# Two stacked transformer blocks on one core: 1/rms of the queries and of the compressed vectors applied behind the products

## Chip, cores and metric

The kernel runs on one core of one Trainium2 chip. The metric is device time in microseconds (us) of one execution. Engines are named as in the profile: PE is TensorE's matrix products, PEld its weight loads, DVE is VectorE, ACT is ScalarE, POOL is GpSimd, SP issues the loads of weights.

## The reference, cut to what matters

Two blocks of two layers each are computed in fp32. The first block has two streams of 256 tokens (context and latent). The change lies in its mixer:

```python
u = h @ w_in
u_q, u_k, u_v, u_cq, u_ckv, u_kr, pool_in = jnp.split(u, offs, axis=-1)
qg = rms_norm(u_q.reshape(b, l, GQA_HEADS, HEAD_DIM), g_q_gqa)          # 6 heads of 64
kg = rms_norm(u_k.reshape(b, l, GQA_KV_HEADS, HEAD_DIM), g_k_gqa)       # 2 heads of 64
qm = (rms_norm(u_cq, g_cq) @ w_uq).reshape(b, l, MLA_HEADS, MLA_QK)     # 256 -> 6 x 96
kv = (rms_norm(u_ckv, g_ckv) @ w_ukv).reshape(b, l, MLA_HEADS, MLA_NOPE + MLA_V)
km = jnp.concatenate([kv[..., :MLA_NOPE], k_rope], axis=-1)
qm, km = rms_norm(qm, g_q_mla), rms_norm(km, g_k_mla)
...            # rotation of latent queries and keys, then
p = softmax(q k^T * scale); o = p v        # GQA heads and MLA heads
```

`rms_norm(x, g)` is x times 1/sqrt(mean(x^2) + eps) times g, per token and head. In layer 0 both streams have queries, in layer 1 only the latent one; keys and values always come from both.

## The kernel before

Activations lie with tokens on the 128 partitions (four tiles: two of context, two latent) and are transposed on TensorE for the next product. Every fp32 weight is loaded by SP into one of five `raw` buffers, split by ScalarE (`wh`, L345) and VectorE (`wl`, L346) into a high and a low part in a ring of four, and each product is three matmuls (`mm3`, L428 to L430) on such parts. Sums go to two PSUM buffers of two banks each (`acc`), transposes and small products to two single banks (`wk`) and one pair (`pr`).

Side work runs as Python generators (`spawn`, `tick`, `drain`): the main line of products calls `tick` after each weight part, and each tick lets the generators issue their next piece. The order of issue is also the priority by which the framework's planner then orders the instructions of each engine; an instruction is placed when its inputs and buffers are ready in the planner's own model of time.

`first_layer` runs for both layers of the first block. `in_group` computes three column groups of the input projection: keys, values and the compressed vectors `ckv` (416 columns), queries (448), compressed queries `cq` (448). Its inner `ev` copies sums from PSUM with ScalarE (L832, L833) to token tiles `u` (`uin` in the profile). Four generators follow:

- `chain_kv`: square sums of each key head (GpSimd squares, L463, VectorE sums, L464) and of `ckv` (ScalarE, L454), the power -1/2 on GpSimd (L436), the multiply of keys (L760) and of `ckv` (L761) by 1/rms, the rotation, the transposes (L775, L776) and the split of `ckv` (`ckr`).
- `chain_q`: the same for the queries: square sums, 1/rms (24 columns in layer 0, by twelve small VectorE operations L439 to L444; 12 columns in layer 1, by GpSimd), multiply L790, rotation or gain (L794), transposes L799, copy L801.
- `chain_cq`: square sums of the compressed queries (L454), 1/rms (L436), multiply L811, transposes L817, the split into `cqr` (L423, L424).
- `chain_km`: up_kv makes keys and values of the MLA heads from `ckr` (copies L874, L876); the chain takes square sums, one 24-column 1/rms, multiplies by it (L889) and by the gain (L895, L893), and transposes (L902).

`latent_queries` makes the MLA queries from `cqr` in two banks for each tile of tokens; `chain_uq` copies them out (L923), squares them (L463), multiplies by 1/rms (L934) and by the gain (L935), rotates and transposes (L945). `attention` runs 18 pairs of heads in layer 0 (six of them with four softmax pieces, twelve with two) and 12 in layer 1 (two pieces each), three pairs deep: scores (L998), the negative maximum (L1008), exponentials with their sum (L1011), reciprocal and scaling (L1013, L1015), transposes (L1024, copy L1027), the product with the values (L1037), the split of the result (`mix`, L419, L420). The second block's attention already scales its scores in the softmax (L1565, L1569).

## Time and profile before

| what | value |
|---|---|
| median of 3 runs | 1771.93 us (1769.02 to 1772.63) |
| the profiled execution | 1766.66 us |
| its span, first to last instruction | 1764.7 us |
| granted TensorE clock, mean of the span | 0.984 of full speed |
| busy: PE, DVE, ACT, POOL | 1694.5, 1025.4, 855.8, 331.6 us |

The prediction works with durations from the one profiled execution; its own time lies 5.27 us under the median of the three runs. In the profile the mixer of layer 0 lies between about 60 and 215 us, that of layer 1 between about 705 and 830 us.

### The profile page before, as it was taken

The page shows a single profiled execution, that of the slowest core. Times are in us where ns is not written, and L with a number is a line of the kernel's source. Part 1 is how long each engine was busy: PE and PEld are TensorE (multiplying, and loading weights), DVE is VectorE, ACT ScalarE, POOL GpSimd, SP SyncE. Part 2 cuts the span into 40 slices and gives each one's busy share as a digit, 9 for nine tenths or more (in the row PEclk, how much of TensorE's full clock was granted, in tenths as well). Part 3 has the DMA queues.
Part 4 walks back from the last instruction along what each step waited for, and adds up shares of the span by engine and source line. Part 5 has one row for each costly group of instructions (what it writes and reads, how often), then busy time and mean ns, then how long its engine had stood idle before and what let it go on. Part 6 is the DMA issues. An engine that isn't in the chain of part 4 may idle for free.

```text
span 1764.7 us, 26533 instructions
## 1 busy us (share of the span) xinstructions
PE 1694.5 (96%) x10062; PEld 1362.7 (77%) x10062; DVE 1025.4 (58%) x1882; ACT 855.8 (48%) x1658; POOL 331.6 (19%) x414
## 2 busy tenths in 40 slices
PE   6989999999999999889999999999999999999998
PEld 5776578777778888656899978877778788787787
DVE  3476634333333436774566778776575577866755
ACT  4556534413222234564544465665554446655542
POOL 1134110211112121331122224520000034300000
PEclk9999999999999999999999999999999999999999
DMA  7611254555443322602665545444355444343453
GB/s 285 211 61 54 74 190 125 179 163 166 149 151 118 96 78 77 219 30 81 218 189 184 188 146 167 138 132 156 119 170 188 145 155 154 129 160 119 155 183 104
DMA packets 71999, 256.23 MB, mean 145 GB/s; under 512 B 8120, under 2 KB 9272, under 8 KB 71616
## 3 DMA queue, kind: packets, MB, share of 16 engines
q1 hardware_dynamic: 71856, 254.53, 44.2%
q8 instruction: 79, 1.29, 0.3%
q14 instruction: 48, 0.39, 0.1%
q10 hardware_dynamic: 16, 0.02, 0.0%
HBM read 253.47 MB, written 1.05 MB: 144 GB/s over the span
## 4 chain that ended last, share of the span: by engine, by line
PE 86%; DVE 6%; ACT 3%; DMA 2%; POOL 2%; issue 1%; SPq 0%; DVEq 0%; ACTq 0%; POOLq 0%
PE acc L428 24%; PE acc L430 23%; PE acc L429 23%; PE acc L998 2%; DVE wl L346 2%; PE pr L549 2%; PE wk L1037 1%; DMA raw<-in_dram 1%; PE pr L1024 1%; ACT e L1011 1%; PE pr L1703 1%; PE wk L549 1%; ACT wh L345 1%; PE pr L1553 1%; DVE nmx L1008 1%
## 5 line engine op out<-in xcount | busy, mean ns | idle before, releaser
L346 DVE TENSOR_TENSOR wl<-raw,wh 128x1024 fp32r<-128x1024 f32 (+3 forms) x384 | 478.7, 1249 | 415.5 <-ACT wh L345 414.9
L345 ACT CAST wh<-raw 128x1024 fp32r<-128x1024 f32 (+3 forms) x384 | 396.7, 1034 | 505.2 <-PE acc L430 338.6
L428 PE MATMUL acc<-wl,hh 128*128 128x512 f32 x576 | 231.1, 401 | 4.6 <-ACT tga L1683 2.3
L429 PE MATMUL acc<-wh,hh 128*128 128x512 f32 x576 | 230.5, 400 | 0.0
L430 PE MATMUL acc<-wh,hl 128*128 128x512 f32 x576 | 229.6, 399 | 0.0
L428 PE MATMUL acc<-wl,hidh 128*128 128x512 f32 x384 | 152.5, 398 | 0.0
L429 PE MATMUL acc<-wh,hidh 128*128 128x512 f32 x384 | 151.2, 394 | 0.0
L430 PE MATMUL acc<-wh,hidl 128*128 128x512 f32 x384 | 151.0, 395 | 0.0
L1197 POOL TENSOR_TENSOR sqr<-relu 128x512 f32<-128x512 f32 (+1 forms) x64 | 72.6, 1135 | 346.5 <-ACT relu L1195 233.1
L428 PEld LDWEIGHTS acc<-wl,hh 128*128 128x128 f32 x576 | 109.5, 190 | 28.2 <-ACT tga L1683 3.2
L430 PEld LDWEIGHTS acc<-wh,hl 128*128 128x128 f32 x576 | 109.5, 190 | 22.8 <-issue 1.3
L429 PEld LDWEIGHTS acc<-wh,hh 128*128 128x128 f32 x576 | 109.5, 190 | 22.2 <-issue 1.3
L428 PE MATMUL acc<-hl,wh 128*128 128x258 f32 (+1 forms) x384 | 113.1, 295 | 3.5 <-DVE xc L1627 3.5
L429 PE MATMUL acc<-hh,wh 128*128 128x258 f32 (+1 forms) x384 | 111.6, 291 | 0.0
L430 PE MATMUL acc<-hh,wl 128*128 128x258 f32 (+1 forms) x384 | 111.0, 290 | 0.0
L428 PE MATMUL acc<-h2l,wh 128*128 128x512 f32 (+1 forms) x288 | 108.4, 376 | 2.7 <-DVE dx L1128 2.7
L429 PE MATMUL acc<-h2h,wh 128*128 128x512 f32 (+1 forms) x288 | 108.5, 377 | 0.0
L430 PE MATMUL acc<-h2h,wl 128*128 128x512 f32 (+1 forms) x288 | 107.5, 373 | 0.0
L428 PEld LDWEIGHTS acc<-wl,hidh 128*128 128x128 f32 x384 | 72.2, 188 | 17.8 <-issue 1.8
L430 PEld LDWEIGHTS acc<-wh,hidl 128*128 128x128 f32 x384 | 72.1, 188 | 17.1 <-issue 1.0
L429 PEld LDWEIGHTS acc<-wh,hidh 128*128 128x128 f32 x384 | 72.2, 188 | 16.4 <-issue 0.8
L1130 POOL TENSOR_TENSOR x<-x,dx 128x512 f32<-128x512 f32 x30 | 45.8, 1553 | 198.1 <-DVE dx L1128 198.1
(425 smaller groups left out, 3343.1 us busy)
## 6 DMA issues: line engine op xcount, KB each, us to landing
raw<-in_dram SPq DMA_DIRECT2D x448, 512.0 KB, 3.6
raw<-in_dram SPq DMA_DIRECT2D x16, 448.0 KB, 4.2
raw<-in_dram SPq DMA_DIRECT2D x8, 416.0 KB, 6.0
x<-in_dram SPq DMA_DIRECT2D x2, 1024.0 KB
band<-in_dram SPq DMA_DIRECT2D x4, 512.0 KB
raw<-in_dram SPq DMA_DIRECT2D x4, 288.0 KB, 4.2
out_dram<-x SPq DMA_DIRECT2D x4, 256.0 KB, 2.0
rows<-in_dram SPq DMA_DIRECT2D x4, 232.0 KB, 2.5
```

Source lines behind the costliest of these rows:

```text
L345: S.copy(h, src)
L346: V.tensor_tensor(l, src, h.bitcast(F32), ALU.subtract)
L428: T.matmul(ps, a[0], b[1], start=start, stop=False)
L429: T.matmul(ps, a[0], b[0], start=False, stop=False)
L430: T.matmul(ps, a[1], b[0], start=False, stop=stop)
L549: T.matmul(ps[32 * j:32 * j + 32, 0:P], cpad[:, k, :], raw[:, k * P:(k + 1) * P], start=a == 0, stop=a == 1)
L998: T.matmul(ps[:, a, s_ * w:(s_ + 1) * w], pr["q"][a][s_], pr["k"][a], start=True, stop=True)
L1008: V.tensor_reduce(nmx, ps.rearrange("p a (q w) -> p (a q) w", q=nq), AX.X, ALU.max, negate=True)
L1011: S.activation(e[:, c * w:(c + 1) * w], pf[:, c * w:(c + 1) * w], AF.Exp, bias=nmx[:, c:c + 1], accum_out=ssum[:, c:c + 1])
L1024: T.transpose(pt[:, a, (k * nq + s_) * P:(k * nq + s_ + 1) * P], d["e"][:, a * 512 + (s_ * nk + k) * P:a * 512 + (s_ * nk + k + 1) * P], i ...
L1130: (V if o else G).tensor_tensor(xs, xs, d, ALU.add)
L1197: G.tensor_tensor(s, t, t, ALU.mult)
```

## The change

1/rms of the queries (GQA and MLA) is no longer multiplied into them. It is kept in `rq` and `rm` and enters the softmax: the negative maximum is multiplied by it, and the exponential takes it as its scale. 1/rms of the compressed queries cancels in the norm of the MLA queries up to the epsilon; it scales the squares of the query products (`rcq`) and the final `rm`. 1/rms of `ckv` (now the last of the columns 33 to 35 of `krs`) is applied where the keys and values are copied out of PSUM. So the transposes of `cq` and `ckv` need only the copies out of PSUM. The nope part of the MLA key gain moves into the query gain `gqm`. Query products are multiplied by `gqm` straight out of PSUM by VectorE, and squares move from GpSimd to ScalarE; the keys' 1/rms of the MLA heads is taken tile by tile on GpSimd. `rsqrt` and `rsqrt_mean` get an argument for the place of the result, and `head_pairs`, `gqa_pairs` and `mla_pairs` hand each pair its columns of `rq` or `rm` as `pr["r"]`.

```diff
-        krs = const.tile([P, 4, 33], F32, tag="krs", name=nm("krs"))
+        krs = const.tile([P, 4, 36], F32, tag="krs", name=nm("krs"))
+        rqs = smp.tile([P, 52], F32, tag="rq", name=nm("rqs"), bufs=1)
+        rq, rm = (rqs[:, a:a + 24].rearrange("p (t h) -> p t h", t=4) for a in (0, 24))
+        rcq = rqs[:, 48:52]
...
+        V.tensor_tensor(gqm[:, 0:64], gqm[:, 0:64], rw("gkm", 96)[:, 0:64], ALU.mult)
...
         def chain_kv(us, j0=0):
...
-                group_ss(s3[:, j - j0, 0:2], u[:, 0:128], 2, u[:, 128:256])
+                group_ss(s3[:, j - j0, 0:2], u[:, 0:128], 2, u[:, 128:256], act=True)
...
-            r = rsqrt(ms.rearrange("p t c -> p (t c)"), 3 * n).rearrange("p (t c) -> p t c", t=n)
+            for j, u in enumerate(us, j0):
+                pt = wk_ps()
+                T.transpose(pt[:, 0:P], u[:, 256:384], ident)
+                scaled_split(ckh[:, j * P:(j + 1) * P], ckl[:, j * P:(j + 1) * P], pt[:, 0:P], gk)
+            r = krs[:, j0:j0 + n, 33:36]
+            G.tensor_tensor(r, s3, nhalf[:, 0:3 * n].rearrange("p (t c) -> p t c", t=n), ALU.pow)
             yield 1
...
-                V.tensor_scalar(u[:, 256:384], u[:, 256:384], r[:, j - j0, 2:3], None, ALU.mult)
...
-                T.transpose(pt[:, P:2 * P], u[:, 256:384], ident)
                 V.tensor_copy(kT[:, j * P:(j + 1) * P], pt[:, 0:P])
-                scaled_split(ckh[:, j * P:(j + 1) * P], ckl[:, j * P:(j + 1) * P], pt[:, P:2 * P], gk)
                 yield 1
+
+        def ev_q(j, ps, u):
+
+            p3 = ps[:, 0:384].rearrange("p (g d) -> p g d", g=6)
+            if tq[j] >= 2:
+                S.copy(u[:, 0:384], ps[:, 0:384])
+            else:
+                V.tensor_tensor(u[:, 0:384].rearrange("p (g d) -> p g d", g=6), p3, gq8.unsqueeze(1).to_broadcast([P, 6, 64]), ALU.mult)
+            S.activation(Bqf[:, j * 384:(j + 1) * 384], ps[:, 0:384], AF.Square)
 
         def chain_q(us):
...
-                group_ss(ss[:, 6 * j:6 * j + 6], u[:, 0:384], 6, Bqf[:, j * 384:(j + 1) * 384])
+                V.tensor_reduce(ss[:, 6 * j:6 * j + 6], Bqf[:, j * 384:(j + 1) * 384].rearrange("p (g d) -> p g d", g=6), AX.X, ALU.add)
             yield 1
-            r = rsqrt_mean(ss, 6 * n, 64)
             for j, u in enumerate(us):
                 u3 = u[:, 0:384].rearrange("p (g d) -> p g d", g=6)
-                V.tensor_tensor(u3, u3, r[:, 6 * j:6 * j + 6].unsqueeze(2).to_broadcast([P, 6, 64]), ALU.mult)
                 if tq[j] >= 2:
                     rope_tok(u3, u3, 6, 32, pair(qs[:, tq[j] - 2, 0, 0, :]), pair(qs[:, tq[j] - 2, 0, 1, :]))
-                else:
-                    G.tensor_tensor(u3, u3, gq8.unsqueeze(1).to_broadcast([P, 6, 64]), ALU.mult)
-                yield 1
+                    yield 1
...
+            rsqrt_mean(ss, 6 * n, 64, rq[:, tq[0]:tq[0] + n, :].rearrange("p t h -> p (t h)"))
 
         def chain_cq(us):
...
-            for j, u in enumerate(us):
-                sumsq(ss[:, j:j + 1], u[:, 0:256], u[:, 256:512])
-            r = rsqrt_mean(ss, n, 256)
-            for j, u in enumerate(us):
-                V.tensor_scalar(u[:, 0:256], u[:, 0:256], r[:, j:j + 1], None, ALU.mult)
-            yield 1
...
+                sumsq(ss[:, j:j + 1], u[:, 0:256], u[:, 256:512])
                 yield 1
+            rsqrt_mean(ss, n, 256, rcq[:, tq[0]:tq[0] + n])
...
-                S.copy(u, pk[:, 0:384])
+                S.activation(u, pk[:, 0:384], AF.Copy, scale=krs[:, t, 35:36])
                 uks.append(u)
-                S.copy(vm[:, t, :], pv[:, 0:384])
+                S.activation(vm[:, t, :], pv[:, 0:384], AF.Copy, scale=krs[:, t, 35:36])
             W.used()
 
         def chain_km():
-            ss = sm(24, "ssm")
+            rs_ = []
             for j, u in enumerate(uks):
-                group_ss(ss[:, 6 * j:6 * j + 6], u, 6)
-                V.tensor_scalar(ss[:, 6 * j:6 * j + 6], ss[:, 6 * j:6 * j + 6], krs[:, j, 32:33], None, ALU.add)
-                yield 1
-            r = rsqrt_mean(ss, 24, 96)
-            yield 2
+                ss = sm(6, "ssm")
+                group_ss(ss, u, 6, act=True)
+                V.tensor_scalar(ss, ss, krs[:, j, 32:33], 1.0 / 96, ALU.add, ALU.mult)
+                V.tensor_scalar(ss, ss, EPS, None, ALU.add)
+                rs_.append(rsqrt(ss, 6))
+                if j % 2:
+                    yield 1
+            yield 1
             for j, u in enumerate(uks):
                 u3 = u.rearrange("p (g d) -> p g d", g=6)
-                V.tensor_tensor(u3, u3, r[:, 6 * j:6 * j + 6].unsqueeze(2).to_broadcast([P, 6, 64]), ALU.mult)
...
-                    V.tensor_tensor(ktok[:, :, 0:64], u3[:, 3 * g2:3 * g2 + 3, :],
-                                    rw("gkm", 96)[:, 0:64].unsqueeze(1).to_broadcast([P, 3, 64]), ALU.mult)
+                    V.tensor_tensor(ktok[:, :, 0:64], u3[:, 3 * g2:3 * g2 + 3, :], r3.to_broadcast([P, 3, 64]), ALU.mult)
...
         def chain_uq(some):
...
-            for t, g2, pq in some:
-                u = ut(288, "uq")
-                S.copy(u, pq[:, 0:288])
+            us, sq = [], []
+            m = sm(6, "msu")
+            for j, (t, g2, pq) in enumerate(some):
+                u, q = ut(288, "uq"), tmp(288, n="squ")
+                V.tensor_tensor(u.rearrange("p (g d) -> p g d", g=3), pq[:, 0:288].rearrange("p (g d) -> p g d", g=3),
+                                gqm.unsqueeze(1).to_broadcast([P, 3, 96]), ALU.mult)
+                S.activation(q, pq[:, 0:288], AF.Square, scale=rcq[:, t:t + 1])
+                V.tensor_reduce(m[:, 3 * j:3 * j + 3], q.rearrange("p (g d) -> p g d", g=3), AX.X, ALU.add)
                 us.append(u)
...
-                V.tensor_tensor(u3, u3, r[:, 3 * j:3 * j + 3].unsqueeze(2).to_broadcast([P, 3, 96]), ALU.mult)
-                G.tensor_tensor(u3, u3, gqm.unsqueeze(1).to_broadcast([P, 3, 96]), ALU.mult)
...
+            r = rsqrt_mean(m, 6, 96)
+            t, g0 = some[0][0], some[0][1]
+            V.tensor_scalar(rm[:, t, 3 * g0:3 * g0 + 6], r, rcq[:, t:t + 1], None, ALU.mult)
...
                 V.tensor_reduce(nmx, ps.rearrange("p a (q w) -> p (a q) w", q=nq), AX.X, ALU.max, negate=True)
+                V.tensor_tensor(pair(nmx), pair(nmx), pr["r"], ALU.mult)
                 pf = ps.rearrange("p a c -> p (a c)")
                 for c in range(2 * nq):
                     S.activation(e[:, c * w:(c + 1) * w], pf[:, c * w:(c + 1) * w], AF.Exp, bias=nmx[:, c:c + 1],
-                                 accum_out=ssum[:, c:c + 1])
+                                 scale=pr["r"][:, c // nq, c % nq:c % nq + 1], accum_out=ssum[:, c:c + 1])
```

## Rows read from the trace of the kernel before

**Rows 1.** The page's part 1: busy us, share of the span, instructions of each engine.

```profile
PE 1694.5 (96%) x10062; PEld 1362.7 (77%) x10062; DVE 1025.4 (58%) x1882; ACT 855.8 (48%) x1658; POOL 331.6 (19%) x414
```

**Rows 2.** Busy time by stretch (us from the span's start) around the mixers.

```profile
core 0: us, PE busy (x) PEld busy (x) DVE busy (x) ACT busy (x) POOL busy (x), PEclk, DMA share, GB/s
...
110.00:140.00 30.00, 25.41 (x165) 18.63 (x162) 21.13 (x62) 18.55 (x64) 9.33 (x14) 0.89 0.15 50
140.00:200.00 60.00, 56.70 (x431) 37.09 (x432) 39.67 (x100) 39.10 (x102) 19.81 (x42) 1.00 0.11 32
121.00:130.00 9.00, 7.89 (x40) 6.29 (x42) 5.49 (x18) 5.71 (x21) 0.46 (x1) 0.62 0.00 0
733.00:780.00 47.00, 36.07 (x243) 24.92 (x235) 39.54 (x94) 31.51 (x75) 21.79 (x33) 0.89 0.24 80
743.00:755.00 12.00, 8.99 (x42) 6.08 (x44) 8.69 (x23) 6.04 (x17) 1.16 (x2) 0.72 0.19 68
760.00:780.00 20.00, 13.80 (x104) 9.44 (x102) 17.33 (x41) 13.61 (x30) 12.35 (x22) 0.91 0.17 54
```

**Rows 3.** Waits of PE, 55 to 270 us: total, times, longest.

```profile
PE wk L817 <- DVE uin L811: 2.3, 1, 2.3
PE acc L428 <- ACT cqr L423: 1.1, 1, 1.1
...
PE acc L428 <- ACT uin L833: 0.5, 1, 0.5
```

**Rows 4.** Waits of PE, 700 to 840 us.

```profile
PE wk L1037 <- DVE mixl L420: 2.8, 1, 2.8
...
PE acc L430 <- DVE cqr L424: 1.6, 1, 1.6
...
PE acc L428 <- ACT ckr L423: 0.9, 1, 0.9
PE wk L817 <- ACT Bq L801: 0.7, 1, 0.7
```

**Rows 5.** Timeline, 114 to 123 us: start, us, instruction, idle before it and releaser.

```profile
114.59 0.38 ACT L833 COPY uin<-acc 128x256 f32<-128x256 f32 x1
...
119.40 1.01 POOL L436 TENSOR_TENSOR rs<-ms,nhalf 128x4 f32<-128x4 f32 x1
...
120.44 1.14 DVE L811 TENSOR_SCALAR uin<-uin,rs 128x256 f32<-128x256 f32 x4
...
120.94 0.67 PE L817 MATMUL wk<-con,uin 128*128 128x128 f32 x4 [2.34 <-DVE uin L811]
```

**Rows 6.** DVE's groups by shape, 705 to 830 us: busy us, mean ns.

```profile
L934 DVE TENSOR_TENSOR uq<-uq,rs 128x288 f32<-128x288 f32 x4 | 1.6, 449 | 0.0
...
L811 DVE TENSOR_SCALAR uin<-uin,rs 128x256 f32<-128x256 f32 x2 | 1.2, 626 | 0.1
...
L889 DVE TENSOR_TENSOR km<-km,rs 128x384 f32<-128x384 f32 x2 | 1.1, 552 | 0.0
...
L444 DVE SCALAR_TENSOR_TENSOR rs<-rt,rs 128x24 f32<-128x24 f32 x3 | 1.0, 327 | 0.1
...
L442 DVE TENSOR_TENSOR rt<-ms,rs 128x24 f32<-128x24 f32 x3 | 0.6, 209 | 0.1
```

**Rows 7.** Groups by shape over the whole span, ACT and DVE.

```profile
L1569 ACT ACTIVATE e<-pr,nmx,rq 128x256 f32<-128x256 f32 x32 | 17.7, 563 | 0.0
...
L1011 ACT ACTIVATE e<-acc,nmx 128x256 f32<-128x256 f32 x24 | 11.1, 474 | 7.6 <-DVE nmx L1008 7.6
...
L833 ACT COPY uin<-acc 128x384 f32<-128x384 f32 x6 | 2.9, 495 | 0.0
...
L1627 DVE TENSOR_TENSOR xc<-acc,rb 128x256 f32<-128x256 f32 x16 | 6.3, 412 | 0.8 <-PE acc L430 0.8
...
L1565 DVE TENSOR_TENSOR nmx<-nmx,rq 128x4 f32<-128x4 f32 x16 | 2.6, 161 | 0.3
```

**Rows 8.** GpSimd's power of six columns, over the whole span.

```profile
L436 POOL TENSOR_TENSOR rs<-ms,nhalf 128x6 f32<-128x6 f32 x6 | 8.8, 1474 | 17.7 <-DVE ms L449 17.7
```

More of the change, by code (lines that the diff above doesn't have):

```diff
@@ L430, in mm3, with rsqrt @@
         T.matmul(ps, a[1], b[0], start=False, stop=stop)
-    def rsqrt(ms, n, tag="sm"):
-        r = sm(n, "rs")
+    def rsqrt(ms, n, r=None):
+        r = sm(n, "rs") if r is None else r
         if n <= 12:
@@ L445, in rsqrt, with rsqrt_mean @@
         return r
-    def rsqrt_mean(ss, n, d):
+    def rsqrt_mean(ss, n, d, r=None):
         m = sm(n, "ms")
         V.tensor_scalar(m, ss, 1.0 / d, EPS, ALU.mult, ALU.add)
-        return rsqrt(m, n)
+        return rsqrt(m, n, r)
     def sumsq(dst, src, junk=None):
@@ L745, in chain_kv @@
             n = len(us)
-            ss = sm(4 * n, "ssk")
+            ss = sm(3 * n, "ssk")
             s3 = ss.rearrange("p (t c) -> p t c", t=n)
+            gk = col(("gckv", i), 1)
             for j, u in enumerate(us, j0):
-                group_ss(s3[:, j - j0, 0:2], u[:, 0:128], 2, u[:, 128:256])
+                group_ss(s3[:, j - j0, 0:2], u[:, 0:128], 2, u[:, 128:256], act=True)
                 sumsq(s3[:, j - j0, 2:3], u[:, 256:384], vm[:, j, 0:128])
                 sumsq(krs[:, j, 32:33], u[:, 384:416], vm[:, j, 128:160])
-            ms = sm(3 * n, "msk").rearrange("p (t c) -> p t c", t=n)
-            V.tensor_scalar(ms[:, :, 0:2], s3[:, :, 0:2], 1.0 / 64, EPS, ALU.mult, ALU.add)
-            V.tensor_scalar(ms[:, :, 2], s3[:, :, 2], 1.0 / 128, EPS, ALU.mult, ALU.add)
-            r = rsqrt(ms.rearrange("p t c -> p (t c)"), 3 * n).rearrange("p (t c) -> p t c", t=n)
+            V.tensor_scalar(s3[:, :, 0:2], s3[:, :, 0:2], 1.0 / 64, EPS, ALU.mult, ALU.add)
+            V.tensor_scalar(s3[:, :, 2], s3[:, :, 2], 1.0 / 128, EPS, ALU.mult, ALU.add)
+            for j, u in enumerate(us, j0):
[4 more added lines that the diff above has]
+            G.tensor_tensor(r, s3, nhalf[:, 0:3 * n].rearrange("p (t c) -> p t c", t=n), ALU.pow)
             yield 1
@@ L820, in chain_cq, with in_group @@
                                  col(("gcq", i), 2)[:, k:k + 1])
+                sumsq(ss[:, j:j + 1], u[:, 0:256], u[:, 256:512])
                 yield 1
+            rsqrt_mean(ss, n, 256, rcq[:, tq[0]:tq[0] + n])
         chains = []
-        def in_group(g, tiles, ncols, w, chain, make, parts):
+        def in_group(g, tiles, ncols, w, chain, make, parts, out=None):
             us = []
@@ L832, in ev @@
                     S.copy(view(tiles[j]), ps[:, c0:c1])
-                S.copy(u[:, 0:w], ps[:, 0:w])
+                if out is None:
+                    S.copy(u[:, 0:w], ps[:, 0:w])
+                else:
+                    out(j, ps, u)
                 us.append(u)
@@ L854, in first_layer @@
         kvs = list(chains)
-        in_group(1, tq, 448, 384, chain_q, free, [(lambda t: pin[:, t, 0:64], 384, 448)])
+        in_group(1, tq, 448, 384, chain_q, free, [(lambda t: pin[:, t, 0:64], 384, 448)], ev_q)
         h_q = chains[-1]
@@ L919, in chain_uq @@
         def chain_uq(some):
-            us = []
-            for t, g2, pq in some:
-                u = ut(288, "uq")
-                S.copy(u, pq[:, 0:288])
+            us, sq = [], []
[6 more added lines that the diff above has]
+                V.tensor_reduce(m[:, 3 * j:3 * j + 3], q.rearrange("p (g d) -> p g d", g=3), AX.X, ALU.add)
                 us.append(u)
-            ss = sm(6, "ssu")
+            yield 1
             for j, u in enumerate(us):
-                group_ss(ss[:, 3 * j:3 * j + 3], u, 3)
-            yield 2
-            r = rsqrt_mean(ss, 6, 96)
-            yield 2
-            for j, u in enumerate(us):
-                t, g2, _ = some[j]
-                u3 = u.rearrange("p (g d) -> p g d", g=3)
-                V.tensor_tensor(u3, u3, r[:, 3 * j:3 * j + 3].unsqueeze(2).to_broadcast([P, 3, 96]), ALU.mult)
-                G.tensor_tensor(u3, u3, gqm.unsqueeze(1).to_broadcast([P, 3, 96]), ALU.mult)
+                t = some[j][0]
                 if t >= 2:
+                    u3 = u.rearrange("p (g d) -> p g d", g=3)
                     rope_tok(u3[:, :, 64:96], u3[:, :, 64:96], 3, 16, pair(mt[:, t - 2, 0, :]), pair(mt[:, t - 2, 1, :]))
-                yield 1
+            r = rsqrt_mean(m, 6, 96)
+            t, g0 = some[0][0], some[0][1]
+            V.tensor_scalar(rm[:, t, 3 * g0:3 * g0 + 6], r, rcq[:, t:t + 1], None, ALU.mult)
             yield 1
@@ L1056, in attention, with head_pairs @@
                 yield 1
[L1058 removed]
+        def head_pairs(base, st, m0, q, k, v, r):
             nk, nq = (4, 1) if st == 0 else (2, 2)
@@ L1065, in head_pairs @@
                                     q=[[q(h, (base + qt + s_) * P) for s_ in range(nq)] for h in hs_],
-                                    k=[k(h, nk * P) for h in hs_], v=[v(h) for h in hs_]))
+                                    k=[k(h, nk * P) for h in hs_], v=[v(h) for h in hs_],
+                                    r=r(ha, base + qt, nq).rearrange("p t a -> p a t")))
             return res
@@ L1414, in second_layer @@
         vA = big(2048, F32, "vA").rearrange("p (t c) -> p t c", t=2)
-        rq = smp.tile([P, 2, 16], F32, tag="rq", name=nm("rq"), bufs=1)
+        rq = smp.tile([P, 52], F32, tag="rq", name=nm("rq"), bufs=1)[:, 0:32].rearrange("p (t h) -> p t h", t=2)
         def chain_qk(us, dst, which, g):
```

11 lines of the change are left out of this document (6 added, 5 removed).

## Prediction

> **What bounds the kernel now.** I read the page's engine table first: TensorE is busy 96% of the span [rows 1]. A change that leaves its products alone can only win what TensorE loses by waiting or at half clock, and only in the stretches that the change touches. So the next view is the busy time by stretch [rows 2]. In the first layer, 110 to 140 us holds 25.4 us of TensorE work (4.6 idle) at a granted clock of 0.89, and 140 to 200 holds 56.7 (3.3 idle) at full clock. In the second layer, 733 to 780 holds 36.1 us (10.9 idle), again at 0.89. Inside these lie the dips: 0.62 over 9 us from 121, 0.72 over 12 us from 743, 0.91 over 20 us from 760. Idle time together is 18.8 us. At 2.4 GHz against 1.2 GHz the clock missing in the three dips is 9 x 0.38 = 3.4, 12 x 0.28 = 3.4 and 20 x 0.09 = 1.8 us of full-speed time. Some 27 us is the ceiling of any such edit, 1.5% of the span.
>
> Third comes what TensorE waited for. In the first layer the long waits are the transposes of the compressed queries behind L811 (2.3 us) and the products behind them (1.1); the others are under a microsecond [rows 3]. In the second layer the largest that the change can reach are: the context product behind `mixl` (2.8), the query products behind `cqr` (1.6), the key and value products behind `ckr` (0.9), the transposes L817 (0.7) [rows 4]. Fourth, the timeline of the first wait: the first projected tile is copied out at 114.6, the square sums, the power on GpSimd (from 119.4) and the four multiplies L811 (from 120.4) follow, and only at 120.9 do the transposes start, 2.34 us late [rows 5]. That chain is what the change takes out of the way.
>
> **The change part by part.**
>
> *Compressed queries, first layer.* The transposes now need the copy out alone. The wait of 2.3 and the 1.1 after it go, at most 3.4 us, at least nothing (if ScalarE, which still copies four tiles and splits them in that stretch, is late next). I take 3.0, near the row, since the first copy is done some 6 us before the transposes start. The dip from 121 follows this wait: if TensorE stays busy there, up to 3.4 us of clock come back. Part of the dip's time TensorE was not the limit, so I take 2.0.
>
> *Compressed vectors and queries, second layer.* `ckr` and `cqr` no longer wait for 1/rms: waits of 0.9, 0.7 and 1.6, together 3.2 [rows 4]. The splits still queue on VectorE behind weight splits, so I take 2.5 (0 to 3.2). The dip from 743 stands on these waits: 0 to 3.4, I take 1.7.
>
> *VectorE in the second layer, 733 to 780.* It is busy 39.5 of 47 us, and 17.3 of 20 in the last stretch [rows 2], where TensorE waits 2.8 us for a VectorE result. Removed [rows 6]: two L811 (2 x 0.63 = 1.3), four L889 (4 x 0.55 = 2.2), the twelve small operations of the 24-wide 1/rms (three at 0.33, the others like L442 at 0.21: 2.9), four L934 (4 x 0.45 = 1.8), in all 8.2. Added [rows 7]: four multiplies of query products out of PSUM (0.41 at 256 columns, by the row L1627, so about 0.45 at 288: 1.8), some eight multiplies of the maxima (0.16 each: 1.3), four small operations for the keys and two for the scale (6 x 0.18: 1.1), in all 4.2. The net is 4.0 us less on VectorE, in a stretch with 6.2 us idle TensorE from 760. I take 2.5 (0 to 6.2).
>
> *Scale in the softmax.* Every pair multiplies its maxima by 1/rms (0.161, the row of the other block's L1565) and each exponential has a scale column as well as a bias: at 256 columns 563 ns (L1569) against 474 (L1011), 89 ns each [rows 7]. The 24 pairs with two exponentials lengthen by 0.34 us, the six with four by 0.52, in all 11.2 us if each pair lay on the path, nothing if none does. Attention is three pairs deep and from 140 to 200 TensorE is 94% busy, which hides it; if that cover were gone, the 18 pairs of the first layer cost 12 x 0.34 + 6 x 0.52 = 7.2. I count five pairs in the second layer's bad stretch: 1.7. The multiply is also a new wait: it stands in VectorE's order and needs 1/rms of the queries; behind it stand the reciprocal, the probabilities, the next maximum and weight splits, and TensorE waits for these. The 1/rms comes from square sums taken at the eviction, well ahead of the first pair, so I add nothing; if it came late, one power costs 1.5 [rows 8].
>
> *Squares on ScalarE.* The query eviction of the first layer gets a Square for each tile, priced like the 384-column copy, 0.5 [rows 7]. TensorE already waits 0.5 us for these banks [rows 3]; two Squares more stand in front of it: 1.0 (0 if the banks come free earlier). The other squares leave GpSimd, as do the 12 multiplies by `gqm`: nothing on the path, because GpSimd is busy only 21.8 of 47 us. The keys' 1/rms moves to it, four powers of 1.5 us in place of VectorE's twelve; free as long as GpSimd is otherwise idle, 1.5 us a tile if not.
>
> *Query products out of PSUM.* Two copies on ScalarE become a multiply on VectorE and a Square on ScalarE on each bank. TensorE needs the pair of banks again for scores. With six tiles in both layers, held longer by nothing up to the 2.8 us that a VectorE result was late in this stretch, that is 0 to 16.8. I take 0.3 a tile, 1.8, since other products are queued in between. No row shows two engines reading one bank. The Trainium skill (PSUM — Partial Sum Buffer, PSUM bank collisions raise a hardware error) says that two engines may not touch one bank and quadrant at once, reads included, so the two reads would run in series. By that rule the hold is one more read, an estimate of 0.5 us a tile and 3.0 in all, and the forecast would be 1765.9.
>
> *Moved.* The transposes of the compressed vectors come before the power; the same count, but a work bank of their own, and no DMA. The gain rows are free earlier, so the next layer's gains load earlier; nothing waits for them. Products are the same in number.
>
> Gains 3.0 + 2.0 + 2.5 + 1.7 + 2.5 = 11.7; costs 1.7 + 1.0 + 1.8 = 4.5; net 7.2 us. The profiled execution took 1766.7 us, 1764.7 of it the span, so it would take 1759.5; it was 5.3 us under the median of the runs. Against that median, 1771.9, the forecast is **1764.7 us**.
>
> **Rivals.** *The queue behind takes over.* The removed waits each have ScalarE or VectorE work next in line (copies of four tiles, weight splits), the gaps only shrink and the clock falls as before: gains 3.0 + 2.5 without the two clock terms and without the VectorE term, against costs 4.5, leave 1.0, so 1771. For it: TensorE's gaps in the second layer have many names, none above 2.8 us. Against it: the first layer's gap hangs on one chain alone.
>
> *Banks held by VectorE (slower).* Each query tile's eviction waits in VectorE's order behind maxima and weight splits; at the 2.8 us of [rows 4] for all six, 16.8 replaces 1.8: 1771.9 - 11.7 + 2.7 + 16.8 = 1779.7. It decides from (11.7 - 2.7) / 6 = 1.5 us a tile. For it: VectorE is 87% busy from 760. Against it: 4.0 us of its work leave, and the first layer's VectorE is two thirds busy.
>
> *All of it.* All waits named go and the clock holds: 3.4 + 3.4 + 3.2 + 3.4 + 6.2 = 19.6 of gains, with costs 4.5: 1756.8.
>
> **How the numbers follow.** About 0.2% (3.5 us) is what a measurement of this kernel can tell from no change. Forecast, 1760 to 1768: 0.50; all of it, under 1760: 0.16; queue behind, within 3.5 us of before: 0.19; banks held, over 1775.5: 0.15. Faster is 0.66, same 0.19, slower 0.15. The range of 8 in 10 goes from 1755, just past the case of all gains with its costs, to 1775, which leaves out the slower case and a little below; the likeliest case's own range is 1760 to 1768.
>
> **What would show it.** Right: no wait of L817 on VectorE in the first layer, the granted clock from 110 to 140 above 0.95, TensorE idle from 733 to 780 under 7 us, VectorE there some 4 us lighter per the same work. Wrong: query or score products waiting for VectorE's new eviction, exponentials waiting for a maximum that waits for 1/rms, the dips at 0.6 to 0.7 still there after the waits are gone, or a reordering by the planner that puts new waits after 200 or after 803 us, where I count nothing.

## The result, and the profile after

The changed kernel takes **1784.4 us** (median of 4 runs, 1783.6 to 1785.6) against 1772.3 of the kernel before on the same chip: ratio 1.0062, 95% interval 1.0046 to 1.0078. It is 0.6% slower; 1764.7 was forecast, with a range up to 1775. The profiled execution took 1783.6 us, its span 1781.8. One run of one kernel below (before + multiply and scale column: 2303.1 us at a granted clock of 0.675) is left out of its median.

The engines over the span, answering to [rows 1]:

```profile
PE 1702.9 (96%) x10062; PEld 1364.6 (77%) x10062; DVE 1004.8 (56%) x1878; ACT 871.3 (49%) x1678; POOL 305.4 (17%) x374
```

VectorE is 20.6 us lighter, GpSimd 26 us, ScalarE 15.5 us heavier: the work moved as the change says. The time moved the other way. By stretch, as in [rows 2]:

```profile
core 0: us, PE busy (x) PEld busy (x) DVE busy (x) ACT busy (x) POOL busy (x), PEclk, DMA share, GB/s
110.00:140.00 30.00, 24.53 (x172) 17.99 (x170) 13.66 (x41) 19.57 (x63) 3.67 (x7) 0.89 0.17 52
140.00:200.00 60.00, 54.26 (x406) 37.62 (x400) 36.42 (x102) 37.26 (x91) 8.79 (x18) 0.97 0.09 27
...
733.00:780.00 47.00, 36.26 (x227) 24.97 (x227) 29.64 (x70) 29.69 (x67) 13.89 (x16) 0.87 0.40 130
```

From 140 to 200 us TensorE now idles 5.7 us instead of 3.3, and its clock fell from 1.00 to 0.97. From 733 to 780 VectorE has 29.6 us of work instead of 39.5, and TensorE idles as long as before (10.7 us against 10.9); layer 1's first query product starts 11.3 us later than before (755.0 against 743.7), so part of the work in this stretch is other work. TensorE's waits, 55 to 270 us and then 690 to 860 us (total, times, longest), as in [rows 3, 4]:

```profile
PE acc L1012 <- ACT e L1026: 7.4, 11, 2.2
PE wk L825 <- ACT km L918: 2.1, 1, 2.1
...
PE acc L428 <- ACT Bq L795: 1.2, 1, 1.2
```

```profile
PE acc L1012 <- ACT e L1026: 5.2, 4, 2.1
...
PE wk L764 <- ACT mrow L550: 2.5, 1, 2.5
...
PE acc L428 <- ACT e L1026: 1.5, 1, 1.5
...
PE wk L825 <- ACT Bq L813: 0.9, 1, 0.9
...
PE acc L430 <- DVE cqr L424: 0.3, 1, 0.3
```

Three waits have new names. The scores (L1012) wait for the exponentials of an earlier pair to free their bank, 12.6 us over both layers; in the kernel before, from 110 to 860 us, it was 1.6:

```profile
PE acc L998 <- ACT e L1011: 1.6, 3, 0.9
```

The transposes of the compressed queries (L825) no longer wait 2.3 us for the multiply but 2.1 us for a ScalarE copy that frees a work bank. The transposes of the compressed vectors (L764) wait 2.5 us for another such copy. The timeline from 196 to 203 us (start, us, instruction, idle before it and its releaser) shows what stands behind the first wait:

```profile
196.82 1.21 DVE L1022 TENSOR_REDUCE nmx<-acc 128x2 f32<-128x1024 f32 x1
...
197.94 0.87 DVE L1030 TENSOR_SCALAR e<-e,rsum 128x512 f32<-128x512 f32 x2
...
198.73 0.42 DVE L420 TENSOR_TENSOR mixl<-wk,mixh 128x256 fp32r<-128x256 f32 x1
199.06 0.47 DVE L424 SCALAR_TENSOR_TENSOR mixl<-wk,cols,mixh 128x256 fp32r<-128x256 f32 x1
199.46 0.15 DVE L1023 TENSOR_TENSOR nmx<-nmx,rqs 128x2 f32<-128x2 f32 x1
...
200.56 0.79 ACT L1026 ACTIVATE e<-acc,nmx,rqs 128x512 f32<-128x512 f32 x1
...
202.25 1.98 PE L1012 MATMUL acc<-km,qm 96*128 96x512 f32 x4 [0.44 <-ACT e L1026]
```

The maximum is done at 198.0. Its multiply, 0.15 us long, starts only at 199.46, behind the probabilities of the pair before (L1030) and a split of the mixer's result (L420, L424). The exponentials start at 200.56, behind a ScalarE copy of 1.0 us that had begun at 199.66, and the next scores at 202.25, when these have read the bank.

### The profile page after: what moved, and what is told of

Its sections match the earlier page's. It is cut to its first block, busy times and chain, and to the rows that moved or that the text cites. A ratio compares the mean times of both kernels' runs of the same rounds, so it can differ in the third digit from the quotient of the medians.

```text
span 1781.8 us, 26481 instructions
## 1 busy us (share of the span) xinstructions
PE 1702.9 (96%) x10062; PEld 1364.6 (77%) x10062; DVE 1004.8 (56%) x1878; ACT 871.3 (49%) x1678; POOL 305.4 (17%) x374
## 4 chain that ended last, share of the span: by engine, by line
PE 85%; DVE 5%; ACT 5%; DMA 2%; POOL 2%; issue 1%; SPq 0%; DVEq 0%; ACTq 0%; POOLq 0%
PE acc L428 24%; PE acc L430 23%; PE acc L429 23%; ACT e L1026 2%; PE pr L549 2%; PE acc L1012 1%; DMA raw<-in_dram 1%; DVE wl L346 1%; PE pr L1039 1%; PE pr L1721 1%; PE wk L549 1%; DVE nmx L1022 1%; PE wk L1052 1%; PE pr L1571 1%; ACT wh L345 1%
## 5 line engine op out<-in xcount | busy, mean ns | idle before, releaser
L430 PE MATMUL acc<-wh,hl 128*128 128x512 f32 x576 | 231.5, 402 | 0.0
L430 PE MATMUL acc<-wh,hidl 128*128 128x512 f32 x384 | 151.6, 397 | 0.0
L430 PEld LDWEIGHTS acc<-wh,hl 128*128 128x128 f32 x576 | 109.3, 190 | 24.2 <-issue 0.7
L430 PE MATMUL acc<-hh,wl 128*128 128x258 f32 (+1 forms) x384 | 110.4, 288 | 0.0
L430 PE MATMUL acc<-h2h,wl 128*128 128x512 f32 (+1 forms) x288 | 107.7, 374 | 0.0
L430 PEld LDWEIGHTS acc<-wh,hidl 128*128 128x128 f32 x384 | 72.1, 188 | 17.7 <-issue 1.4
```

Of the source, the lines that this page charges most:

```text
L430: T.matmul(ps, a[1], b[0], start=False, stop=stop)
```

## The experiments

Each time is compared with the kernel before on the same chip. "Wait" is TensorE's wait of the scores for exponentials, from 110 to 860 us, in the one profile of each kernel; a few microseconds of it are without effect (4.1 and 4.7 at a ratio of 1.000). "Attention" is the time of two stretches of that profile together: in layer 0 from the first query product to the first product of the layer's MLP, in layer 1 from the first query product to the last product of the mixer's output. Two profiles of the kernel before agree in it within 0.3 us, while their whole times are 6.4 us apart.

| kernel | us, median | ratio to before, 95% interval | wait, us | attention, us |
|---|---|---|---|---|
| before, first profile | 1771.9 | | 1.6 | 247.6 |
| before, again | 1774.5 | 1.0001 (0.9985 to 1.0018) | 2.5 | 247.9 |
| changed | 1784.4 | 1.0062 (1.0046 to 1.0078) | 12.6 | 254.0 |
| changed, multiply of the maxima dead | 1778.4 | 1.0021 (1.0007 to 1.0035) | 7.2 | 243.2 |
| changed, no multiply | 1778.3 | 1.0023 (1.0010 to 1.0036) | 7.5 | 243.3 |
| changed, no multiply, no scale column | 1779.5 | 1.0034 (1.0020 to 1.0049) | 4.6 | 244.4 |
| changed, multiply on GpSimd | 1782.2 | 1.0050 (1.0032 to 1.0067) | 9.4 | 245.0 |
| changed, query products copied by ScalarE | 1780.2 | 1.0036 (1.0021 to 1.0050) | 9.4 | 246.1 |
| changed, VectorE alone reads them | 1784.5 | 1.0054 (1.0034 to 1.0074) | 9.4 | 248.1 |
| changed, copied by ScalarE, no multiply, no scale | 1774.9 | 1.0011 (0.9996 to 1.0026) | 3.7 | 236.8 |
| changed, longer pauses | 1797.7 | 1.0153 (1.0126 to 1.0180) | 8.6 | 257.2 |
| before + multiply and scale column | 1782.2 | 1.0059 (1.0036 to 1.0082) | 5.9 | 256.7 |
| before + dead multiply | 1772.3 | 0.9989 (0.9977 to 1.0002) | 1.9 | 248.3 |
| before + eviction of the query products | 1781.2 | 1.0048 (1.0031 to 1.0065) | 4.0 | 253.1 |
| before + compressed queries | 1779.2 | 1.0033 (1.0014 to 1.0051) | 4.0 | 251.6 |
| before + the same, pause kept | 1773.4 | 0.9998 (0.9983 to 1.0013) | 4.7 | 245.9 |
| before + compressed vectors | 1779.5 | 1.0032 (1.0015 to 1.0049) | 4.3 | 247.8 |
| before + both, pauses as changed | 1781.7 | 1.0046 (1.0027 to 1.0065) | 3.7 | 252.4 |
| before, two pauses shortened | 1784.9 | 1.0062 (1.0042 to 1.0082) | 3.6 | 252.3 |
| before, another pause taken out | 1773.8 | 0.9997 (0.9979 to 1.0015) | 4.1 | 247.0 |

**The softmax scale.** Taken out of the changed kernel as a whole (the multiply's line goes too):

```diff
-                                 scale=pr["r"][:, c // nq, c % nq:c % nq + 1], accum_out=ssum[:, c:c + 1])
+                                 accum_out=ssum[:, c:c + 1])
```

> The changed kernel without 1/rms of the queries in the softmax: the maxima are not multiplied and the exponentials have no scale column (the queries stay unscaled). All the rest of the change stays. Theory 'queue': the stretch from the end of the query products to the first context product of the first layer, 9.3 us longer after the change than before, falls back by 6 to 9 us, the second layer's by 3 to 5, and the time is 1770 to 1775. Theory 'banks': only the 89 ns of an exponential come back, 2 to 5 us, 1779 to 1782, and the multiplies of the query products still end some 8 us after their products.

Then put alone into the kernel before:

```diff
+                V.tensor_tensor(nmx, nmx, ones[:, 0:2 * nq], ALU.mult)
...
+                                 scale=ones[:, c:c + 1], accum_out=ssum[:, c:c + 1])
```

> The kernel before, with a multiply of the maxima by ones in VectorE's order and a scale column of ones on each exponential, and nothing else of the change (its result is that of the kernel before). Theory 'queue': slower by 6 to 13 us, 1778 to 1785, the scores of the next pair waiting for exponentials that wait for the multiply. Theory 'banks': slower by 2 to 5 us (the length of the exponentials only), 1774 to 1777. My own forecast of before had 1.7 us for this.

The first fell to 1.0034, the second rose to 1.0059: some 0.3% to 0.6% on either kernel. Next the multiply was parted from the scale column and then made dead, written to a tile that nothing reads, in both kernels:

```diff
-                V.tensor_tensor(pair(nmx), pair(nmx), pr["r"], ALU.mult)
+                V.tensor_tensor(pair(sm(2 * nq, "dead")), pair(nmx), pr["r"], ALU.mult)
```

> The changed kernel with the scale column kept on every exponential (a column of ones in place of 1/rms, the same length) and without the multiply of the maxima: 1/rms of the queries is left out of the softmax. The kernel without either took 4.9 us less than the changed one. Theory 'place in the queue': most of that comes back, 1779 to 1781, and the exponentials start right behind the maxima. Theory 'length' (72 exponentials, 89 ns each, lengthen the loop of score bank, maximum, exponential): nothing to 1 us comes back, 1783 to 1785.

> The changed kernel with the multiply of the maxima in its place on VectorE, but written to a small tile that nothing reads; the exponentials take the maxima as they are and a column of ones as scale (1/rms of the queries is left out of the softmax). Theory 'wait': as good as without the multiply (which took 0.4% less than the changed kernel), 1777 to 1780. Theory 'load or order': no better than the changed kernel, 1782 to 1786.

> The kernel before with a multiply of the maxima by ones in VectorE's order, written to a small tile that nothing reads (30 operations, 4.7 us of VectorE in all; the result is unchanged, no exponential waits for it, no scale column). Theory 'wait' (exponentials wait for the multiply's place): within 2 us of before, 1772 to 1775. Theory 'order' (any edit moves the planner's order off a favourable one): as slow as the multiply that is waited for, 1778 to 1783.

These settle the multiply's length and its load on VectorE. VectorE does the same 30 operations when they are dead, and the time is that of the kernel without them (1.0021 beside 1.0023; TensorE, ScalarE and GpSimd run the same instructions in the same order in these two). On the kernel before the dead multiply costs nothing (0.9989). What costs is that the exponentials depend on it. The row of the live multiply in the changed kernel and that of its dead twin (count, min/median/max ns):

```profile
L1023 DVE TENSOR_TENSOR nmx<-nmx,rqs x30: 147/154/257, 121.1 to 821.1; 128x2 f32<-128x2 f32 x24, 128x4 f32<-128x4 f32 x6
...
who waited for it (us, times):
  ACT e L1026: 22.1, 15
```

```profile
L1023 DVE TENSOR_TENSOR dead<-nmx,rqs x30: 148/155/164, 122.1 to 807.2; 128x2 f32<-128x2 f32 x24, 128x4 f32<-128x4 f32 x6
...
who waited for it (us, times):
  PEld wk L1052: 0.8, 1
```

30 x 0.155 = 4.7 us in either. The exponentials wait 22.1 us for the live multiply; with the dead one they wait for the maximum itself, for 14.7 us. Live and then dead, from 110 to 860 us:

```profile
ACT e L1026 <- DVE nmx L1023: 22.1, 15, 2.3
```

```profile
ACT e L1026 <- DVE nmx L1022: 14.7, 12, 5.7
...
PE acc L1012 <- ACT e L1026: 7.2, 10, 1.8
```

The score wait falls from 12.6 to 7.2 us. Against the kernel before, each on its own chip, the changed kernel takes 12.1 us more and the one with the dead multiply 5.2: the live multiply costs some 7 us, 0.41% of the time, give or take 0.2 points by the two intervals. The difference lies where the exponentials are. Layer 0's first query products and the first products of its MLP, live and then dead (first and last start):

```profile
L428 PE MATMUL acc<-wl,cqr x16: 289/350/602, 124.4 to 165.4; 128*128 128x288 f32 x16
...
L429 PE MATMUL acc<-h2h,wh x288: 276/391/800, 285.8 to 641.6; 128*128 128x512 f32 x112, 128*128 128x256 f32 x32
```

```profile
L428 PE MATMUL acc<-wl,cqr x16: 289/294/404, 125.4 to 161.2; 128*128 128x288 f32 x16
...
L429 PE MATMUL acc<-h2h,wh x288: 276/393/800, 278.9 to 635.0; 128*128 128x512 f32 x112, 128*128 128x256 f32 x32
```

That is 161.4 against 153.5 us; over both layers the attention takes 254.0 live and 243.2 dead. On the kernel before it takes 256.7 with the live multiply and scale column, 248.3 with the dead multiply and 247.6 without. One thing the dead twin does not part: making the multiply live changes the order as well. From 126 us on the order of VectorE's other instructions differs between live and dead in some 70 places. How much of the 7 us is the wait itself and how much the order that follows from it stays open; on the kernel before, the score wait grows by 4 us (1.9 to 5.9) where the attention grows by 8.4. The scale column, 89 ns on each exponential, costs nothing that these runs tell: without it, 1.0034 is no lower than 1.0023 with it.

The multiply on GpSimd (`G.` for `V.`), which sat idle until the maximum was done for 21 of the 30:

> The changed kernel with the multiply of the maxima on GpSimd, which is idle 80% of the span, in place of VectorE; all else as it is, the result too. Theory 'place in the queue': the multiply no longer stands behind probabilities and weight splits, but pays two hand-overs and GpSimd's own duration of maybe 0.3 to 0.5 us: 1780 to 1784. Theory 'length': 1784 to 1788, since a hand-over is added to a loop that was not waiting in VectorE's order.

```profile
L1023 POOL TENSOR_TENSOR nmx<-nmx,rqs x30: 194/202/368, 121.4 to 814.1; 128x2 f32<-128x2 f32 x24, 128x4 f32<-128x4 f32 x6
...
  DVE nmx L1022: 72.8, 21
...
  ACT e L1026: 16.9, 15
```

It takes 0.20 us, the score wait falls by 3.2 us and the attention to 245.0 us, near the dead multiply's 243.2; but this is one profile, of the fastest of seven runs, and the ratio, 1.0050, can't be told from the changed kernel's 1.0062.

**The query products.** Copies on ScalarE in the changed kernel, and the change's eviction alone in the kernel before:

```diff
-                V.tensor_tensor(u.rearrange("p (g d) -> p g d", g=3), pq[:, 0:288].rearrange("p (g d) -> p g d", g=3),
-                                gqm.unsqueeze(1).to_broadcast([P, 3, 96]), ALU.mult)
-                S.activation(q, pq[:, 0:288], AF.Square, scale=rcq[:, t:t + 1])
+                S.copy(u, pq[:, 0:288])
...
+                S.activation(q, u, AF.Square, scale=rcq[:, t:t + 1])
+                V.tensor_tensor(u3, u3, gqm.unsqueeze(1).to_broadcast([P, 3, 96]), ALU.mult)
```

> The changed kernel, but the query products are copied out of PSUM by ScalarE alone (both banks, as before the change), and the Square and the multiply by the gain read the copy in SBUF. Everything else of the change stays. Theory 'banks' (the pair of banks is held 4.4 to 8.4 us because two engines read it in turns): TensorE's wait from the query products to the end of that stage goes, about 1 to 3 us a layer come back, 1778 to 1781. Theory 'queue' (the multiply of the maxima waits in VectorE's order, and the next scores with it): the banks cost little, the two long multiplies move from PSUM to SBUF at about the same length, so within 2 us of 1784.4. Theory 'order' (the planner's other order alone): any time between 1772 and 1786, with no wait that names the query products.

> The kernel before, with its query products taken out of PSUM by a multiply on VectorE and a Square on ScalarE, as the change does, and nothing else of it: the 1/rms is still multiplied into the queries. Theory 'banks': slower by 3 to 8 us, 1775 to 1780, products of the query stage or scores waiting for that multiply. Theory 'queue': within 2 us of 1772. My forecast of before had 1.8 us for this, with 16.8 as its upper bound.

The first gave back some 5.6 us (from 12.1 to 6.5 above the kernel before on the same chip), the second cost 7.5 us. The changed kernel's first tile, whose products end at 130.3:

```profile
130.47 0.45 DVE L939 TENSOR_TENSOR uq<-acc,gqm 128x288 f32<-128x288 f32 x1
...
134.24 0.51 ACT L941 ACTIVATE squ<-acc,rqs 128x288 f32<-128x288 f32 x1
134.78 0.46 DVE L939 TENSOR_TENSOR uq<-acc,gqm 128x288 f32<-128x288 f32 x1 [1.34 <-ACT squ L941]
...
137.88 0.50 ACT L941 ACTIVATE squ<-acc,rqs 128x288 f32<-128x288 f32 x1 [0.29 <-DVE msu L942]
```

The two engines read the pair of banks strictly in turns, the second bank's multiply waiting for the first bank's Square, and the pair is held until 138.4, 8.1 us. Over the six tiles it takes 3.7 to 10.7 us from the first read to the end of the last, where ScalarE's two copies in the kernel before take 0.7 to 1.1. To see whether that hold is the cost, VectorE alone reads PSUM (`AF.Square` takes `u`):

> The changed kernel with VectorE alone reading the query products out of PSUM: its multiply stays, and the Square on ScalarE reads the multiplied copy in SBUF (so the square sums are those of the gained products, another number). Theory 'turns' (two engines read one pair of banks in turns, each waiting for the other): as good as the copies by ScalarE, 1779 to 1781, the second multiply following the first within a microsecond. Theory 'VectorE's queue' (the multiply itself comes late, whoever else reads): no better than the changed kernel, 1783 to 1786.

```profile
134.65 0.81 DVE L939 TENSOR_TENSOR uq<-acc,gqm 128x288 f32<-128x288 f32 x2
...
140.08 0.55 ACT L941 ACTIVATE squ<-uq,rqs 128x288 f32<-128x288 f32 x1
```

Both banks are read in 0.81 us and the Square comes later, out of SBUF, yet the time stays at 1.0054. So the theory of turns is not borne out: with the long hold gone, the whole time is no better. It is not refuted either: the attention falls from 254.0 to 248.1 us, other stretches of this profile are longer, and VectorE's order differs from the changed kernel's from 131 us on. That ScalarE's copies help the changed kernel stands at the edge of what the intervals part (1.0021 to 1.0050 against 1.0046 to 1.0078).

**Neither.** Both suspected costs out of the changed kernel:

> The changed kernel without its two suspected costs: query products copied out by ScalarE alone, and no 1/rms of the queries in the softmax (neither multiply nor scale column; that part of the computation is left out). What remains is the rest of the change: transposes before 1/rms, squares on ScalarE, keys' 1/rms four times on GpSimd, and the other order of the planner. If the two costs add (4.2 + 4.9 us), 1775 to 1776, that is 1 to 3 us above the kernel before, and the gains that I forecast (11.7 us) are not there at all. Theory 'the gains are there, the two costs ate them': 1764 to 1770, below the kernel before.

It runs at 1.0011, not told from before. So the rest of the change as a whole neither wins nor loses. One profile each shows where: from the first query product to the first product of the layer's MLP it takes 125.5 to 277.5 = 152.0 us (155.7 before, 122.7 to 278.4), and in the second layer from the first query product to the last of the mixer's output 750.6 to 835.4 = 84.8 (91.9 before, 743.7 to 835.6). Together 10.8 us are gained. But the first query product of layer 0 starts 2.8 us later, layer 0's MLP up to layer 1's first product takes 2.5 us longer (408.8 against 406.3), and the second layer's input stage 5.3 us longer (64.3 against 59.0); the second profile of the kernel before, below, has 155.6, 92.3, 406.4 and 60.8 for the four. The later start need not be the edit's: the kernel before with the dead multiply has its instructions in the order of the kernel before up to 690 us, and its first query product starts 1.9 us later too (124.6). The pattern is not this kernel's alone: the changed kernel with the multiply dead, taken out or on GpSimd has a shorter attention than the kernel before (243.2 to 245.0 us against 247.6) and takes longer as a whole (1.0021 to 1.0050). The waits of the changed kernel without both costs in layer 1's input stage, 686 to 748 us:

```profile
PE acc L428 <- ACT uin L844: 3.6, 1, 3.6
...
PE wk L584 <- DVE ssm L898: 1.4, 1, 1.4
```

**The compressed vectors and queries alone.** In the kernel before, transposes and split ahead of 1/rms, which goes on as the scale of ScalarE's copies behind the products:

> The kernel before, with one part of the change alone: the compressed queries are transposed and split before their 1/rms is known, and the 1/rms goes on behind the products, as the scale of the two copies on ScalarE that take the query products out of PSUM (the result is that of the kernel before; the four multiplies, two on the path, and their place ahead of the transposes are gone). Theory 'gains are there' (my forecast: 3.0 + 2.0 in the first layer, about 1.6 + part of the 1.7 in the second): faster by 5 to 7 us, 1766 to 1769. Theory 'the next in line takes over' (ScalarE's and VectorE's queues set these starts): within 2 us of before, 1772 to 1776, with the transposes waiting for an earlier ScalarE copy in place of the multiply.

> The kernel before, with another part of the change alone: the compressed vectors are transposed and split before 1/rms, which goes on as the scale of the copies of the key and value products. Theory 'gains are there' (my forecast: 0.9 + 0.7 of waits and part of the clock): faster by 1 to 3 us, 1770 to 1772. Theory 'the next in line takes over': no change, or 2 to 3 us slower, with the transposes waiting some 2.5 us behind a ScalarE copy for their bank in the second layer, as in the changed kernel.

> The kernel before, with both of these parts and nothing else: no multiply of maxima, no second reader of the query products, no Squares in the eviction. If the gains that I forecast are there and add, faster by 6 to 10 us, 1763 to 1768; if the queue behind takes over, within 3 us of before.

All three were slower, by 0.32% to 0.46%, more than either theory had. With the compressed vectors the transposes wait in the second layer for a ScalarE copy that frees their bank, as L764 does in the changed kernel:

```profile
PE wk L758 <- ACT mrow L550: 2.1, 1, 2.1
```

With the compressed queries the first wait of layer 0 did go, from 2.3 to 0.6 us. With them came a pause taken out of their generator, as in the change. It was put back, all else kept:

```diff
             ss = sm(n, "ssc")
+            yield 1
             for j, u in enumerate(us):
```

> The kernel before with the compressed queries transposed ahead of their 1/rms, as in the run of that part alone, but with the tick in front of the transposes kept, so that they are issued at the same place as before. Theory 'the pause moved the order' (the two shortened pauses of the query generator alone cost 0.62% on this kernel): at or below the kernel before, 1765 to 1772, the wait of 2.3 us in the first layer gone. Theory 'the next in line takes over': still 1776 to 1781, about 1 us gained ahead of the first query product and more lost behind it.

At 0.9998 the loss is gone, and there is no gain. Its waits from 112 to 165 us, and the stretch 112 to 126, where the kernel before has TensorE busy 10.1 us at a clock of 0.84:

```profile
PE acc L428 <- ACT cqr L423: 1.6, 1, 1.6
...
PE wk L813 <- ACT km L902: 0.6, 1, 0.6
```

```profile
112.00:126.00 14.00, 11.33 (x69) 9.00 (x68) 10.51 (x33) 8.79 (x33) 4.61 (x8) 1.00 0.12 39
```

The transposes wait 0.6 instead of 2.3 us, now for a copy of keys that frees their bank, and the products behind them 1.6 instead of 1.1: of 3.4 us of waits 2.2 stay. From the last input product to the first query product it takes 6.6 us (118.0 to 124.6) against 7.7 (115.0 to 122.7).

**Pauses alone.** If a pause can cost 0.33%, so can others. The change shortens two in the query generator (`yield 2` to `yield 1`, twice). That alone in the kernel before, a different pause taken out there, and longer pauses in the changed kernel:

> The kernel before, with two pauses of the query generator shortened from two ticks to one, as the change has them: same instructions, other order. Theory 'order': 5 to 8 us slower than before, 1778 to 1781. Theory 'each part its own cost': within 2 us, 1771 to 1775.

> The kernel before, with the pause in the middle of the generator of keys and compressed vectors taken out: same instructions, other order. Theory 'order': 5 to 8 us slower than before, 1778 to 1781. Theory 'each part its own cost': within 2 us, 1771 to 1775.

> The changed kernel with the pauses of the query generator given back: two ticks after the products are taken out of PSUM, and two more in front of 1/rms. Same instructions, other order. Theory 'pauses' (the shortened pauses are the change's own loss, as on the kernel before, where they cost 0.62%): 1773 to 1778. Theory 'wait' (the multiply that is waited for, and the eviction by VectorE, 0.4 and 0.3%): within 3 us of the changed kernel, 1782 to 1787. Both at work: 1778 to 1782.

The same instructions in another order cost 0.62%, nothing, and from 1.0062 to 1.0153 another 0.9%. The longest of the new waits with the two shortened pauses, 684 to 848 us:

```profile
PE pr L1024 <- DVE e L1015: 5.3, 3, 3.5
```

The transposes of the probabilities wait for VectorE; before, that wait was not among those of 0.2 us or more. With the two shortened pauses the loss is in layer 1's attention, 96.8 us against 91.9. The theory that any edit throws the kernel off a lucky order falls too, by the dead multiply, the pause taken out and the compressed queries with their pause, all at 0.999 to 1.000. Some orders cost, and which do was not to be seen ahead of the run.

**The control.**

> The kernel before, unchanged: how far two series of one kernel stand apart, and a second profile of it, since the profiled execution shown before was some 6 us under its median. Ratio 1.000 within 0.0015; in the profile, the stretches up to the second layer's products and the second block some 2 to 5 us longer than in the first one.

1.0001; the second profile is 6.4 us longer than the first, 3.5 of it in the second block, though every engine runs the same instructions in the same order.

## Why the prediction was wrong

Forecast was 7.2 us less, measured 12.1 us more: a miss of 19.3 us. Two steps failed. The larger part, 12 us, is that the gains were added up as if each were a gain of the whole; 5 us are the softmax scale, where the place of its multiply was put at nothing; some 4 us are the query products, mis-sized (the three need not add up exactly).

- **Softmax scale: a step that failed.** The forecast gave it 1.7 us for the length of five pairs and, for the place of the multiply, "so I add nothing". The queue behind it was named, but only a late 1/rms was counted as a price. The trace has no wait for 1/rms by the multiply or the exponentials; that they depend on the multiply was the price: some 7 us on the changed kernel, by the dead multiply. The length, which got the 1.7, costs nothing measurable. A pair needs its bank from scores to exponentials, and the maximum stands in that chain; an operation put between takes its place in VectorE's order, here behind 1.4 us of probabilities and splits. That this wait, and not the order that the planner makes of it elsewhere, is all of the 7 us is not shown.
- **The gains as a sum: the step that failed most.** 11.7 us were forecast, 10.7 with the Squares paid. Without the two costs above the change stands at 1.0011 (0.9996 to 1.0026), 1.3 us above the kernel before. One profile shows 10.8 us less behind the first query products of both layers. That it is near the sum is luck: the waits for L811 and `cqr` in the first layer and for `ckr` in the second, which the forecast counted as gained, lie ahead of those products, and there the time grew. 10.6 us are given back: ahead of the first query product, in layer 0's MLP, in layer 1's input stage; and behind layer 1's mixer it is 6.0 us longer (1.7 against the second profile of the kernel before). That fits the rival "the queue behind takes over", at more places than it named. What makes these stages longer stays open.
- **Compressed queries, first layer, 3.0.** Measured alone: 1.1 us ahead of the first query product, and no change in the whole (0.9998). The wait passed to the copy of keys next in ScalarE's order and to the split.
- **Compressed vectors and queries, second layer, 2.5.** The waits of 0.9, 0.7 and 1.6, 3.2 together, became none, 0.9 (L825) and 0.3 (L430), but the transposes of the compressed vectors now wait 2.5 (L764): 3.7 together.
- **The clock.** The stretch 112 to 126 is at 1.00, the 2.4 GHz level, in the run with the pause kept, as forecast, and at 0.84 before. It brought no measurable time. In the changed kernel 110 to 140 still has 0.89. In the second layer 743 to 755 had 0.72, and the stretch 754 to 766, later as the work is, has 0.86; 760 to 780 had 0.91, and 771 to 791 has 0.83.
- **VectorE lighter, 2.5.** It became lighter by more than the 4.0 us forecast: from 744 to 791 us, the same 47 us shifted as the work is, it is busy 31.2 us against 39.5. TensorE idles 11.8 us there against 10.9, so the lighter load alone did not shorten its gaps.
- **Query products, 1.8.** Out of the changed kernel some 5.6 us, alone on the kernel before 7.5 us: over the forecast, under the 16.8 of its bound. The Trainium skill (PSUM — Partial Sum Buffer, PSUM bank collisions raise a hardware error) says that two engines may not access one bank and quadrant at once, reads included, so the two reads of a bank would run in series; the prediction's estimate for that was 3.0 us in all. The trace agrees that they do: in all six tiles multiply, Square, multiply and Square follow one another (the first from 130.47 to 138.38 us), in turns even across the two banks. But one reader alone did not shorten the whole time, so that the hold is the cause is not shown. Whether it is the hold, the order in VectorE's queue or the planner's order after the edit stays open.
- **Squares, 1.0.** The wait for L795 is 1.2 us where L833 was waited for 0.5 [rows 3]: 0.7 more, near the term.
- **What was left out.** The pauses. The change alters the pauses of four generators beside the arithmetic, and the forecast took the order as given. Two of these alone cost 0.62% on the kernel before, a third, in the generator of the compressed queries, 0.33%. On the changed kernel longer pauses are worse by 0.9%, so they can't simply be added: how much of the 12 us is order and how much the two costs stays open beyond the some 7 us that come with the live multiply.

No run was faster than the kernel before beyond its interval.

## What to carry to other kernels

An operation of 0.15 us put into a chain that holds a buffer can cost more than its length, here some 7 us for 30 of them that take 4.7 and cost nothing when no one waits for them. Before pricing it, read what the engine has ready at that moment; test it with a dead twin that does the same work and releases nothing, and compare the order of the other instructions in the two traces, because the dependency may move that too. Where a planner orders the instructions by the order of issue, a changed pause is a change of its own, worth 0% to 0.9% here: move the arithmetic first with the pauses kept, and time that. A stage that gets shorter is no gain until the stages before and after it are read too.

## What the runs showed of the hardware

The first input products, on code that no kernel here edits, run at another granted clock from profile to profile. In the stretch from 28 to 32 us of the second profile of the kernel before, and of the kernel before with the dead multiply, whose instructions stand in the same order up to 690 us:

```profile
28.00:32.00 4.00, 3.69 (x22) 3.39 (x22) 3.72 (x12) 3.86 (x12) 0.00 (x0) 1.00 0.66 246
```

```profile
28.00:32.00 4.00, 4.00 (x15) 3.66 (x14) 3.67 (x11) 3.34 (x10) 0.00 (x0) 0.50 0.54 198
```

The clock is 1.00 (2.4 GHz) in one and 0.50 (1.2 GHz) in the other, after 18 us in which TensorE was busy for 11.3 and 11.8 us at a mean clock of 1.00 and 0.92. A second such stretch follows from 48 to 56 us (0.67 and 0.57). By the first product of the compressed vectors the two are 2.1 us apart (88.1 and 90.2), as much as several terms of the forecast, while their times differ by 0.1%: one profile does not settle a term of that size.
